# Low parts of the second layer's attention weights on GpSimd: one instruction of full width, or two of half width

## The chip, the cores and the metric

The kernel runs on one core of one Trainium2 chip. The metric is the device time of one execution in microseconds (us); three runs of the kernel before gave 1139.0, 1139.27 and 1141.51 us, with a median of 1139.27. The core has five engines that run their own instruction queues in order and wait for one another by semaphores: TensorE (PE, matmuls and transposes), VectorE (DVE), ScalarE (ACT), GpSimd (POOL), and SyncE (SP), which issues most DMAs.

## The reference

Two layers work on 512 tokens of width 1024. Each layer norms its input, projects it (`w_in`), mixes tokens, adds four heads of cross-attention into 256 memory tokens, projects back (`w_out`), and ends with a gated feed-forward part. The first layer mixes by retention, the second by differential attention, six heads with two softmaxes each:

```python
h = rms_norm(x, attn_norm_w[layer])
u = h @ w_in[layer]
# layer 1: q, k (6 heads, 2 x 64), v (6 heads, 128), qc (4 memory heads)
sc = q k^T * scale - slope * |t - s|           # masked by chunks of 64
p = softmax(sc)                                # per head: two maps
o = rms_norm((p[0] - lam * p[1]) @ v, diff_subln_w)
o_mem = memory_attention(qc, mk, mv)
x = x + concat(o, o_mem) @ w_out[layer]
x = x + (silu(gate) * up) @ w_down[layer]      # feed-forward
```

All inputs and weights are float32.

## The kernel before

TensorE is fed with numbers of reduced precision (`fp32r`). To keep the accuracy of float32, each operand is kept as two tiles, a high part H (a rounded copy) and a low part L (the rest), and each product is three matmuls: H·H, H·L, L·H (`mm3`). A weight is loaded by SP into a tile `wr` of 128x1024 (three buffers, `load_chunk`), ACT copies it into `wh`, and another engine writes `wl` = `wr` - `wh`. Three buffers each of `wh` and `wl` hold three such chunks.

Which engine makes the low part is decided in `split_chunk`: VectorE for most weights, GpSimd for the chunks of the second layer's `w_in` (20 of them) and the first five of its `w_out`. One of these five lies in two tiles of 768 and 256 columns, so GpSimd has 26 such instructions, nearly all 128x1024. When the low part is out, the chunk is put into `staged`, from which the matmul code takes it, and the load of the chunk three further on is issued.

GpSimd also computes the reciprocal roots of the norms (`power`, an instruction on 4 or 8 columns, in the profile `sm<-sm,mhalf`), which stand in the same queue.

In the second layer's attention (`diff_layer`), PE's main line is the projection of blocks of 512 tokens with one chunk of weights after the other. Between these matmuls side streams place their work: the norm of queries and keys (ACT square, DVE sum, GpSimd root, DVE product, PE transpose, ACT and DVE split into H and L), the scores (`ps<-qk,qk`), their softmax (a fused DVE pass over each of the two score banks, two ACT exponentials, a DVE combination `wk<-wk,sm,wk`), its transposes (`ps<-ident,wk`), the product with v (`ps<-wk,v`), and at the end of a head its norm and transpose (`ps<-ident,zo`), after which ACT writes the head's H tile and DVE its L tile. The output projection (`out_proj`) takes heads 0 to 3 first, then the memory heads, then heads 4 and 5.

The order of all instructions is fixed when the program is built. A planner (`Weave`) keeps a modelled clock for each engine. Each stream is a Python generator: when it yields, it is put back into a heap with a due time (by default `W.cur`, the modelled end of what it has issued plus a hand-over), and whenever PE's modelled clock has passed a due time, that stream goes on and emits its next instructions. If PE's code asks for something that isn't there yet (`Store.at`), the planner steps the side streams until it is, and only then emits PE's next matmul. A different due time of one stream therefore reorders the streams after it, on all engines. All instructions have the same line in the profile (289), since a helper emits them; they are told apart by tile names: `ps` is a PSUM bank, `wk` a work tile, `qk` a query, key or head tile, `zo` a head's output while it is normed, `sm` a few columns of sums.

Of the kernel before, what the change touches and what calls it, by code (L numbers as in the profile page):

```python
# [15 lines left out]
ALU = mybir.AluOpType  # L16
# [278 lines left out]
def body(ctx: ExitStack, tc: tile.TileContext, x_d, mem_d, w_d, par_d, dec_d, ali_d, out_d):  # L295
# [4 lines left out]
    W = Weave()  # L300
    V, A, G = Engine(W, "dve", nc.vector), Engine(W, "act", nc.scalar), Engine(W, "pool", nc.gpsimd)
# [9 lines left out]
    def page(tag, shape, bufs, dt=F32):  # L311
        z = sb.tile(shape, dt, tag=tag, name=nm(tag), bufs=bufs)
        W.page(tag, bufs, region(z[:, 0:1])[0])
        return z
# [60 lines left out]
    def f(ap):  # L375
        return ap.bitcast(F32)
# [54 lines left out]
    def split_h(dH, src, scale=None):  # L431
        if scale is None:
            A.activation(dH, src, AF.Copy)
        else:
            A.activation(dH, src, AF.Copy, scale=scale)

    def split_l(dH, dL, src, scale=None):
        if scale is None:
            V.tensor_tensor(dL, src, f(dH), op=ALU.subtract)
        else:  # L440
            V.scalar_tensor_tensor(dL, src, scale, f(dH), op0=ALU.mult, op1=ALU.subtract)
# [38 lines left out]
    def load_chunk(i):  # L480

        if i in loaded or i >= RING:
            return
        n = SPECS[i][4] * len(SPECS[i][5])
        raw = page("wr", [P, CW], 3)
        parts = 2 if i < 4 else 1
        cuts = [slice(j * n // parts, (j + 1) * n // parts) for j in range(parts)]
        for s in cuts:
            DMA.dma_start(raw[:, s], w_d[i][:, s])
            if i == 0:  # L490
                DMA.dma_start(xT[cuts.index(s)], x_d[cuts.index(s)])
        loaded[i] = raw, cuts, n
# [3 lines left out]
    def begin(i):  # L496

        if i not in begun and i < RING and SPECS[i][0][0] != "st":
            begun.add(i)
            if i < 3:  # L500
                load_chunk(i)
            W.add(split_chunk(i))

    def split_chunk(i):
        while i not in loaded:
            yield 0.3
        raw, cuts, n = loaded[i]
        key = SPECS[i][0]
        d = key[2] - NOUT + 1 if key[0] == "out" else -1
        if d in (0, 1):  # L510

            while (key[1], d) not in left:
                yield 0.5
            tag, n_page, bufs = (("qc", CW, 2), ("v", MAIN, 8))[d]
        else:
            tag, n_page, bufs = None, CW, 3
        if n_page < n:
            cuts = [slice(0, n_page), slice(n_page, n)]
        pages = [[page(tag or z, [P, n_page], bufs, F32R) for z in ("wh", "wl")] for _ in range(-(-n // n_page))]
        W.cur = max(W.ready(raw[:, 0:1]), W.ready(pages[0][0][:, 0:1]) - 0.2)  # L520
        yield
        for s in cuts:
            wH, wL = [z[:, s.start % n_page:(s.stop - 1) % n_page + 1] for z in pages[s.start // n_page]]
            split_h(wH, raw[:, s])
            yield
            if key[1] == 1 and (key[0] == "in" or key[0] == "out" and key[2] <= NOUT):
                G.tensor_tensor(wL, raw[:, s], f(wH), op=ALU.subtract)
            else:
                split_l(wH, wL, raw[:, s])
        kk, w = SPECS[i][4], n // SPECS[i][4]  # L530
        staged[i] = [[pages[k * w // n_page][j][:, k * w % n_page:k * w % n_page + w] for k in range(kk)] for j in range(2)]
        load_chunk(i + 3)
# [1216 lines left out]
```

## Time and profile before

| | us |
|---|---|
| median of three runs | 1139.27 |
| profiled execution, its device time | 1139.37 |
| its span from first to last instruction | 1137.3 |
| PE busy in the span | 1127.1 (99%) |
| DVE busy | 852.4 (75%) |
| ACT busy | 624.6 (55%) |
| POOL busy | 215.6 (19%) |

The span and what lies around it (2.07 us) make the device time. The ends of matmuls in the records are modelled, so two matmuls that follow one another overlap in the list, and the rate of PE is read from start to start. The granted TensorE clock is full in all of the span. The second layer's attention, with its output projection, lies between about 560 and 760 us; the feed-forward part of the first layer ends before it, that of the second follows.

### The profile page before, as it was taken

To read this page: it belongs to the slowest core of one execution; us is meant where nothing else is said; L and a number is where in the kernel's file an instruction comes from. 1 tells how busy PE (TensorE), PEld (TensorE's weight loads), DVE (VectorE), ACT (ScalarE), POOL (GpSimd) and SP (SyncE) were. 2 spreads that over 40 slices of the span, in tenths; PEclk is the share of its full clock that TensorE was granted. 3 is DMA by queue.
4 is the path that set the end of the run, shared out by engine and by line. 5 is a ranking of instruction groups with operands and counts; after the bars stand their busy time and mean duration, and the time that the engine had idled before them with its cause. 6 is when DMAs were issued, how large, how long until landed. Compare 5 with 4: busy or idle time off the path is not lost.

```text
span 1137.3 us, 18765 instructions
## 1 busy us (share of the span) xinstructions
PE 1127.1 (99%) x6917; PEld 996.6 (88%) x6917; DVE 852.4 (75%) x1648; ACT 624.6 (55%) x1291; POOL 215.6 (19%) x174
## 2 busy tenths in 40 slices
PE   9999999999999999999999999999999999999998
PEld 7788888889999999998888777888899999999987
DVE  6769895788886677877557587957989877677862
ACT  6557863545564445555466566746555544455541
POOL 0120010311111011100353553344111111001100
PEclk9999999999999999999999999999999999999999
DMA  6341122357775566654231321122656766556532
GB/s 227 130 148 65 47 93 82 119 135 199 198 206 160 167 157 176 172 149 160 77 109 56 112 75 50 45 74 93 175 167 172 214 170 184 149 162 181 151 111 76
DMA packets 68491, 153.42 MB, mean 135 GB/s; under 512 B 7728, under 2 KB 20400, under 8 KB 68400
## 3 DMA queue, kind: packets, MB, share of 16 engines
q1 hardware_dynamic: 57312, 132.28, 35.6%
q0 software_dynamic: 10944, 19.93, 11.0%
q8 instruction: 54, 0.88, 0.3%
q14 instruction: 37, 0.30, 0.1%
q10 hardware_dynamic: 144, 0.03, 0.0%
HBM read 150.10 MB, written 2.10 MB: 134 GB/s over the span
## 4 chain that ended last, share of the span: by engine, by line
PE 91%; ACT 3%; DVE 3%; issue 1%; DMA 0%; SPq 0%; DVEq 0%; ACTq 0%
PE ps L289 91%; DVE wk L289 1%; ACT wk L289 1%; ACT wh L289 1%; DVE sm L289 1%; ACT qk L289 1%; DVE qk L289 0%; DMA wr<-w_t 0%; ACT mkY L289 0%; DVE mkL L289 0%; SPq L289 0%; ACT tab L289 0%; ACT qc L289 0%; ACT L289 0%; ACT xw L289 0%
## 5 line engine op out<-in xcount | busy, mean ns | idle before, releaser
L289 PE MATMUL ps<-xw,wh 128*128 128x256 f32 (+1 forms) x1032 | 211.6, 326 | 0.0
L289 ACT ACTIVATE wk<-ps 128x256 f32<-128x256 f32 (+3 forms) x214 | 90.5, 426 | 184.1 <-PE ps L289 183.2
L289 PE MATMUL ps<-xw,wl 128*128 128x256 f32 (+1 forms) x948 | 179.0, 306 | 0.0
L289 PEld LDWEIGHTS ps<-xw,wh 128*128 128x128 f32 x1032 | 154.4, 190 | 15.5
L289 POOL DMA_DIRECT2D wk<-w_t x76 | 67.8, 1002 | 463.8 <-DMA wk<-w_t 176.0
L289 PE MATMUL ps<-wh,xw 128*128 128x512 f32 (+1 forms) x512 | 149.1, 370 | 1.0 <-DVE qk L289 1.0
L289 PEld LDWEIGHTS ps<-xw,wl 128*128 128x128 f32 x948 | 131.2, 190 | 7.4
L289 PE MATMUL ps<-qk,wl 128*128 128x512 f32 (+1 forms) x528 | 135.6, 386 | 0.0
L289 ACT ACTIVATE wh<-wr 128x512 fp32r<-128x512 f32 (+1 forms) x144 | 118.7, 827 | 28.6 <-PE ps L289 16.3
L289 DVE TENSOR_TENSOR wl<-wk,wl 128x512 fp32r<-128x512 f32 (+3 forms) x150 | 94.2, 628 | 41.3 <-ACT wl L289 40.8
L289 DVE TENSOR_TENSOR wh<-wk,wh 128x512 fp32r<-128x512 f32 (+3 forms) x130 | 79.2, 609 | 48.7 <-ACT wh L289 48.5
L289 PEld LDWEIGHTS ps<-qk,wl 128*128 128x128 f32 x528 | 96.1, 188 | 18.3
L289 PE MATMUL ps<-v,wh 128*128 128x256 f32 x792 | 106.1, 279 | 0.0
L289 PEld LDWEIGHTS ps<-wh,xw 128*128 128x128 f32 x512 | 91.5, 188 | 15.8 <-DVE qk L289 1.4
L289 PE MATMUL ps<-qk,wh 128*128 128x512 f32 (+1 forms) x393 | 104.3, 387 | 0.5 <-DVE qk L289 0.5
L289 ACT ACTIVATE wl<-wk 128x512 fp32r<-128x512 f32 (+3 forms) x150 | 85.5, 570 | 31.0 <-DVE wk L289 17.0
L289 PEld LDWEIGHTS ps<-v,wh 128*128 128x128 f32 x792 | 98.3, 189 | 0.0
L289 PE MATMUL ps<-wl,xw 128*128 128x512 f32 (+1 forms) x256 | 94.9, 371 | 0.4 <-DVE wl L289 0.4
L289 DVE TENSOR_TENSOR xT<-ps,xT 128x512 f32<-128x512 f32 (+1 forms) x81 | 55.1, 681 | 51.7 <-PE ps L289 51.4
L289 ACT ACTIVATE wh<-wk 128x512 fp32r<-128x512 f32 (+3 forms) x130 | 72.6, 558 | 34.1 <-DVE wk L289 24.6
L289 PEld LDWEIGHTS ps<-qk,wh 128*128 128x128 f32 x393 | 71.9, 188 | 15.6 <-DVE qk L289 1.1
L289 PE MATMUL ps<-v,wl 128*128 128x256 f32 x576 | 77.4, 279 | 0.0
(169 smaller groups left out, 1956.5 us busy)
## 6 DMA issues: line engine op xcount, KB each, us to landing
wr<-w_t SPq DMA_DIRECT2D x148, 512.0 KB, 3.6
wk<-w_t SPq DMA_DIRECT2D x108, 256.0 KB, 4.0
wk<-w_t POOLq DMA_DIRECT2D x76, 256.0 KB, 6.1
wk<-w_t SPq DMA_DIRECT2D x48, 192.0 KB, 4.6
wk<-w_t SPq DMA_DIRECT2D x32, 128.0 KB, 4.4
wr<-w_t SPq DMA_DIRECT2D x8, 256.0 KB, 5.1
xT<-x_t SPq DMA_DIRECT2D x8, 256.0 KB, 5.1
zo<-mem_t SPq DMA_DIRECT2D x8, 256.0 KB, 5.0
```

The costliest lines, as they stand in the source:

```text
L289: return call(out, *args, **kw)
```

## The change

Each low part that GpSimd makes is written by two instructions, each on half of the columns. After each half the stream yields until the modelled end of that half, so other streams may place instructions between the halves and behind them, and the chunk is put into `staged` (and the load of the chunk three further on is issued) after the modelled end of the second half, where before both came with the instruction's issue.

```diff
             split_h(wH, raw[:, s])
             yield
             if key[1] == 1 and (key[0] == "in" or key[0] == "out" and key[2] <= NOUT):
-                G.tensor_tensor(wL, raw[:, s], f(wH), op=ALU.subtract)
+
+                for j in range(2):
+                    z = slice(j * wL.shape[1] // 2, (j + 1) * wL.shape[1] // 2)
+                    G.tensor_tensor(wL[:, z], raw[:, s][:, z], f(wH)[:, z], op=ALU.subtract)
+                    W.cur = W.last
+                    yield
             else:
                 split_l(wH, wL, raw[:, s])
```

The order changes from the second layer's first input chunk on and is the same again, but for tile numbers, from the fifth output tile of that layer's `w_out` to the end. PE's list has as many matmuls as before; GpSimd's has 26 instructions more. Three places follow, near the end of the attention, where the last heads and the output projection meet.

The first is GpSimd's queue there, before: `wl_1610_7952` is the low part of the first output chunk, `wl_1696_8343`, `qc_1700_8347` and `wl_1698_8345` are those of the next three, and `sm` rows with 128x4 are roots of head norms.

```order
L289 TENSOR_TENSOR wl_1610_7952<-wr_1509_7598,wh_1609_7951 128x1024
L289 TENSOR_TENSOR sm_1601_7930<-sm_1600_7929,mhalf_73 128x8
L289 TENSOR_TENSOR sm_1622_7974<-sm_1621_7973,mhalf_73 128x8
L289 TENSOR_TENSOR sm_1674_8251<-sm_1673_8250,mhalf_73 128x4
L289 TENSOR_TENSOR wl_1696_8343<-wr_1539_7712,wh_1695_8342 128x1024
L289 TENSOR_TENSOR qc_1700_8347<-wr_1628_8013,qc_1699_8346 128x1024
L289 TENSOR_TENSOR wl_1698_8345<-wr_1574_7858,wh_1697_8344 128x1024
L289 TENSOR_TENSOR sm_1740_8512<-sm_1739_8511,mhalf_73 128x4
```

The same place in GpSimd's queue of the changed kernel, where `wl_1608_7966`, `wl_1708_8391`, `qc_1712_8395` and `wl_1710_8393` are these chunks:

```order
L289 TENSOR_TENSOR wl_1608_7966<-wr_1507_7608,wh_1607_7965 128x512
L289 TENSOR_TENSOR sm_1612_7980<-sm_1611_7979,mhalf_73 128x8
L289 TENSOR_TENSOR wl_1608_7966<-wr_1507_7608,wh_1607_7965 128x512
L289 TENSOR_TENSOR sm_1630_8080<-sm_1629_8079,mhalf_73 128x4
L289 TENSOR_TENSOR sm_1695_8360<-sm_1694_8359,mhalf_73 128x4
L289 TENSOR_TENSOR wl_1708_8391<-wr_1526_7700,wh_1707_8390 128x512
L289 TENSOR_TENSOR qc_1712_8395<-wr_1641_8133,qc_1711_8394 128x512
L289 TENSOR_TENSOR wl_1708_8391<-wr_1526_7700,wh_1707_8390 128x512
L289 TENSOR_TENSOR wl_1710_8393<-wr_1595_7925,wh_1709_8392 128x512
L289 TENSOR_TENSOR qc_1712_8395<-wr_1641_8133,qc_1711_8394 128x512
L289 TENSOR_TENSOR wl_1710_8393<-wr_1595_7925,wh_1709_8392 128x512
L289 TENSOR_TENSOR sm_1739_8510<-sm_1738_8509,mhalf_73 128x4
```

Three whole subtractions in a row became six halves in a row, halves of two chunks alternate, and a root now stands between the halves of the first output chunk.

The second place is PE where the first output tile takes head 3, before: `ps_1691_8326<-ident_66,zo_1669_8237` (20 rows ahead of the first of these) was that head's transpose, and `qk_1693_8338` and `qk_1694_8339` are its H and L tiles; `ps_1720_8402` and `ps_1721_8403` are score banks of the last head.

```order
L289 MATMUL ps_1720_8402<-qk_1617_7959,qk_1613_7955 128x384
L289 MATMUL ps_1721_8403<-qk_1617_7959,qk_1613_7955 128x384
L289 MATMUL ps_1720_8402<-qk_1618_7960,qk_1613_7955 128x384
L289 MATMUL ps_1721_8403<-qk_1618_7960,qk_1613_7955 128x384
L289 MATMUL ps_1720_8402<-qk_1617_7959,qk_1614_7956 128x384
L289 MATMUL ps_1721_8403<-qk_1617_7959,qk_1614_7956 128x384
L289 MATMUL ps_1692_8336<-qk_1625_8002,wh_1609_7951 128x512
L289 MATMUL ps_1692_8336<-qk_1624_8001,wl_1610_7952 128x512
L289 MATMUL ps_1692_8336<-qk_1693_8338,wh_1609_7951 128x512
L289 MATMUL ps_1692_8336<-qk_1694_8339,wh_1609_7951 128x512
L289 MATMUL ps_1692_8336<-qk_1693_8338,wl_1610_7952 128x512
```

The same place on PE in the changed kernel, with head 3's transpose in the second row (`zo_1686_8333`), its tiles `qk_1723_8460` and `qk_1724_8461`, and the score banks `ps_1728_8466` and `ps_1729_8467` of the last head:

```order
L289 MATMUL ps_1718_8442<-ident_66,wk_1673_8264 128x128 x3
L289 MATMUL ps_1719_8447<-ident_66,zo_1686_8333 128x128 x4
L289 MATMUL ps_1702_8383<-qk_1664_8232,wl_1608_7966 128x512
L289 MATMUL ps_1728_8466<-qk_1591_7913,qk_1587_7909 128x512
L289 MATMUL ps_1729_8467<-qk_1591_7913,qk_1587_7909 128x512
L289 MATMUL ps_1728_8466<-qk_1592_7914,qk_1587_7909 128x512
L289 MATMUL ps_1729_8467<-qk_1592_7914,qk_1587_7909 128x512
L289 MATMUL ps_1728_8466<-qk_1591_7913,qk_1588_7910 128x512
L289 MATMUL ps_1729_8467<-qk_1591_7913,qk_1588_7910 128x512
L289 MATMUL ps_1730_8478<-ident_66,wk_1720_8454 128x128 x4
L289 MATMUL ps_1702_8383<-qk_1723_8460,wh_1607_7965 128x512
L289 MATMUL ps_1702_8383<-qk_1724_8461,wh_1607_7965 128x512
```

Before, 27 rows of other work stood between the head's transpose and the first use of its tiles; now eight do, six of them the scores of the last head.

The third place is DVE's queue at the same point, before, where `qk_1694_8339` is head 3's L tile and an `ISA` row with `tab` is the fused pass over a score bank:

```order
L289 SCALAR_TENSOR_TENSOR wk_1660_8210<-wk_1661_8211,sm_1679_8269,wk_1660_8210 128x512
L289 RECIPROCAL sm_1686_8290<-sm_1686_8290 128x1
L289 SCALAR_TENSOR_TENSOR sm_1687_8291<-s0_1682_8278,der_89,sm_1686_8290 128x1
L289 SCALAR_TENSOR_TENSOR wk_1683_8279<-wk_1684_8280,sm_1687_8291,wk_1683_8279 128x128
L289 SCALAR_TENSOR_TENSOR qk_1694_8339<-ps_1691_8326,der_89,qk_1693_8338 128x512
L289 ISA wk_1683_8279,sm_1701_8351<-ps_1704_8354,tab_1627_8007 128x256
```

And in the changed kernel, with `qk_1724_8461` as head 3's L tile:

```order
L289 TENSOR_TENSOR zo_1686_8333<-ps_1682_8303,sm_1695_8360 128x512
L289 SCALAR_TENSOR_TENSOR v_1196_6271<-ps_1666_8235,r_1182_6214,v_1195_6270 128x256
L289 RECIPROCAL sm_1714_8400<-sm_1714_8400 128x1
L289 SCALAR_TENSOR_TENSOR sm_1715_8401<-s0_1672_8263,der_89,sm_1714_8400 128x1
L289 SCALAR_TENSOR_TENSOR wk_1703_8385<-wk_1704_8386,sm_1715_8401,wk_1703_8385 128x384
L289 SCALAR_TENSOR_TENSOR sm_1731_8483<-s0_1631_8088 128x4
L289 ISA wk_1705_8387,sm_1725_8463<-ps_1728_8466,tab_1622_8033 128x512
L289 ISA sm_1725_8463 128x1
L289 ISA wk_1706_8388,sm_1725_8463<-ps_1729_8467,tab_1622_8033 128x512
L289 ISA sm_1725_8463 128x1
L289 TENSOR_TENSOR wk_1722_8457<-ps_1718_8442,wk_1721_8456 128x384
L289 SCALAR_TENSOR_TENSOR qk_1724_8461<-ps_1719_8447,der_89,qk_1723_8460 128x512
```

Now the fused passes over the score banks `ps_1728_8466` and `ps_1729_8467` and one more subtraction stand ahead of head 3's L tile.

## Rows read from the trace of the kernel before

**Rows 1.** Page, busy time, share of the span and instructions of each engine.

```profile
PE 1127.1 (99%) x6917; PEld 996.6 (88%) x6917; DVE 852.4 (75%) x1648; ACT 624.6 (55%) x1291; POOL 215.6 (19%) x174
```

**Rows 2.** Busy time by stretch: stretch, PE, PEld, DVE, ACT, POOL, clock, DMA, GB/s.

```profile
130.00:520.00 390.00, 390.00 (x2529) 355.68 (x2529) 305.09 (x556) 207.18 (x406) 50.77 (x50) 1.00 0.55 152
...
560.00:760.00 200.00, 197.40 (x1178) 162.57 (x1177) 142.52 (x371) 127.25 (x316) 93.50 (x52) 1.00 0.25 80
```

**Rows 3.** PE's waits from 560 to 760 us: total, times, longest.

```profile
PE ps L289 <- DVE qk L289: 1.0, 1, 1.0
PE ps L289 <- DVE wk L289: 0.7, 2, 0.5
PE ps L289 <- ACT wk L289: 0.6, 3, 0.2
PE ps L289 <- ACT sm L289: 0.2, 1, 0.2
```

**Rows 4.** Timeline of PE: start, us, instruction, in brackets idle time and releaser.

```profile
654.72 0.44 PE L289 MATMUL ps<-ident,wk 128*128 128x128 f32 x2 [0.15 <-DVE wk L289]
...
679.12 0.40 PE L289 MATMUL ps<-wl,xw 128*128 128x512 f32 x1
679.35 0.40 PE L289 MATMUL ps<-wh,xw 128*128 128x512 f32 x1
680.74 0.50 PE L289 MATMUL ps<-wh,xw 128*128 128x512 f32 x1 [1.00 <-DVE qk L289]
...
742.26 0.96 PE L289 MATMUL ps<-qk,qk 64*128 64x512 f32 x6
743.15 1.57 PE L289 MATMUL ps<-wk,v 128*128 128x256 f32 x12
...
745.54 0.60 PE L289 MATMUL ps<-ident,wk 128*128 128x128 f32 x4
745.89 0.48 PE L289 MATMUL ps<-zo,wl 128*128 128x512 f32 x1
...
755.55 0.65 PE L289 MATMUL ps<-ident,wk 128*128 128x128 f32 x4
...
759.96 0.60 PE L289 MATMUL ps<-ident,zo 128*128 128x128 f32 x4
```

**Rows 5.** GpSimd's groups by form, 560 to 760 us: shapes, count | busy, mean ns | idle.

```profile
L289 POOL TENSOR_TENSOR wl<-wr,wh 128x1024 fp32r<-128x1024 f32 x23 | 55.2, 2400 | 67.1 <-ACT wh L289 67.1
...
L289 POOL TENSOR_TENSOR tab<-tab,tab 128x512 f32<-128x512 f32 x1 | 1.3, 1295 | 3.5 <-ACT tab L289 3.5
```

**Rows 6.** Timeline of GpSimd, two places.

```profile
676.83 2.39 POOL L289 TENSOR_TENSOR wl<-wr,wh 128x1024 fp32r<-128x1024 f32 x1
...
741.65 2.41 POOL L289 TENSOR_TENSOR qc<-wr,qc 128x1024 fp32r<-128x1024 f32 x1
744.00 2.41 POOL L289 TENSOR_TENSOR wl<-wr,wh 128x1024 fp32r<-128x1024 f32 x1
```

**Rows 7.** Timeline of DVE, at and near those places.

```profile
653.92 0.22 DVE L289 SCALAR_TENSOR_TENSOR sm<-s,der,sm 128x1 f32<-128x1 f32 x1
...
678.22 1.02 DVE L289 SCALAR_TENSOR_TENSOR sm<-s,der,sm 128x1 f32<-128x1 f32 x1
...
679.94 0.75 DVE L289 SCALAR_TENSOR_TENSOR qk<-ps,der,qk 128x512 fp32r<-128x512 f32 x1
...
743.13 0.95 DVE L289 SCALAR_TENSOR_TENSOR sm<-s,der,sm 128x1 f32<-128x1 f32 x1
744.12 2.58 DVE L289 SCALAR_TENSOR_TENSOR wk<-wk,sm,wk 128x256 f32<-128x256 f32 x1
...
746.62 0.68 DVE L289 CUSTOM_DVE_ANT_0 wk<-ps,tab 128x512 f32<-128x512 f32 x1
...
748.89 0.55 DVE L289 TENSOR_TENSOR wk<-ps,wk 128x384 fp32r<-128x384 f32 x1
```

## The prediction, made before the changed kernel ran

> **What bounds the kernel now.** I read the page first: PE is busy for 1127.1 of 1137.3 us [rows 1], so all its idle time is 10.2 us, and no change on another engine can give more. Then the busy time by stretch: from 130 to 520 us, the feed-forward part of the first layer, PE is never idle, while the second layer's attention, 560 to 760 us, has 2.6 us of idle PE (200 less 197.40) [rows 2]. The change touches only that stretch, so what it gives or takes is what happens to those 2.6 us. PE's waits there are seven, 2.5 us in sum: one of 1.0 for a DVE tile, two for DVE's work tiles, three of about 0.2 for ACT, one of 0.2 [rows 3]. The bracket of a wait understates it, since matmul ends are modelled: from 679.35 to 680.74 is 1.39 us, where the matmul before had 0.23 (679.12 to 679.35), so this wait cost 1.16, not 1.00 [rows 4]. With about 0.17 more for each of the seven, the stretch holds some 3.7 us of waits. That is the most the change could give back. POOL is busy for 93.5 of the 200 us [rows 2], and PE waits for it nowhere [rows 3].
>
> **The change part by part.** *GpSimd's own time.* 26 subtractions become 52. A full one takes 2.40 us; one of 512 columns is shown by a sum of norms, 1.295 [rows 5]. Two halves are 2.59, so 0.19 more for each pair and 4.9 us for 26. This lies on an engine that is idle for half of the stretch and for which PE never waits. A chunk's low part is due two chunks ahead of its use, and a chunk is 24 matmuls of 0.23 [rows 4], so 11 us of cover for 2.6 us of work. I cost it at 0; if that cover were gone, one chunk would cost at most a half, 1.3. The loads behind the halves go out about 2.6 us later, three chunks (16 us) ahead of need: also 0.
>
> *DVE behind GpSimd.* In the trace some DVE instructions last until a GpSimd instruction ends. The small product `sm<-s,der,sm` takes 0.22 alone (653.92), but the one at 678.22 took 1.02 and ended at 679.24, just when the subtraction of 676.83 + 2.39 ended, at 679.22 [rows 6, 7]. That is 0.80 lost on DVE, and the tile that PE waits for at 680.74 is the DVE row of 679.94, which ends at 680.69, two instructions further down that queue [rows 4, 7]. With halves such a stop ends at 1.3 at the latest, where it was 2.4. The Trainium skill states this as a rule (page "SBUF — State Buffer", section "SBUF: two separate sides"): a port pair shared by VectorE and GpSimd goes to one of them for a whole instruction, and the other is shut out. The trace agrees, with the 1.02 against 0.22 above; by the rule alone the halves would only help.
>
> *The reordering.* This is the larger part, since the due times have moved. I followed the orders past the waits of before.
> - At 680.74 PE began a new bank that DVE had still to empty. In the new order the four new banks of that block come after the old scores, with more work between a bank's last reader and its reuse. I take this wait as gone: -1.2; bounds -1.2 and 0.
> - At 654.72 PE waits 0.15, with the cost of restarting about 0.3, for the softmax of the first head, two tiles of 256 columns; the new order puts about 0.9 us more of PE work between these scores and their transposes: -0.3; bounds -0.3 and 0.
> - The three small waits for ACT are transposes of a finished head right behind six scores, and in the new order two of them stand in the same place and a third a little closer. The two early waits for the memory queries move, but DVE's queue before them moves as well. 0 for all; bounds -1.5 and +1.0.
> - New is the place in the output projection where PE takes head 3. Between the head's transposes and its first use now stand a projection matmul, the six scores of the last head and four transposes. PE takes the H tile in order, and then needs the L tile `qk_1724_8461`. On DVE this tile stands behind both fused passes over these very scores and one subtraction of 384 columns. From the end of the scores: 0.1 until DVE starts, 2 x 0.61 for the passes (0.68 each in the row, less the overlap of records), 0.47 for the subtraction (0.55 in the row), 0.75 for the tile, 0.05 to PE: 2.6 [rows 7]. PE in that time has four transposes, 0.35 (745.54 to 745.89), and one matmul of 0.23: 0.6 [rows 4]. It waits 2.0. Before, 27 rows stood there and PE did not wait. Bounds 1.0 (if an earlier wait of PE takes part of it) and 2.9.
> - Ahead of it, head 3's transpose needs DVE's product `zo_1686_8333`, which stands behind a combination of two work tiles, and this now meets the six halves of GpSimd. Such a combination was held to 2.58 at 744.12, by the subtraction of 744.00 [rows 6, 7]. A half holds it for 1.3 at most, 0.65 in the middle. The last head's norm has one matmul less to hide behind than before: its chain took 755.55 to 759.96 with no wait [rows 4], so 0.2. Together +0.8; bounds 0 and 2.8.
>
> The sum is -1.2 - 0.3 + 0 + 2.0 + 0.8 = +1.3 us. Against the profiled execution's own time of 1139.37 this is 1140.7. That execution lies 0.1 above the median of the runs shown, which I leave in.
>
> **Rivals.** *Halves give more than the order takes.* DVE is freed sooner everywhere; head 3's tile comes as DVE's queue is ahead, and the waits of before go. For it: 24 long subtractions in this stretch and several DVE rows held by them. Against it: only one of PE's seven waits is traced to such a row, and the passes ahead of head 3's tile follow scores, not GpSimd. It gives up to 3.7: with two thirds of that, 2.5, the time is 1136.9.
>
> *DVE held twice at the output projection.* Six halves in a row occupy GpSimd for 6 x 1.3 = 7.8 us, and two combinations of work tiles (`wk_1673_8264`, `wk_1703_8385`) stand on DVE ahead of head 3's product and L tile. If each is held for a whole half, the two cost 2.6 where I counted 0.65, which makes +3.2 and 1142.6. From 0.9 us more than I counted the kernel is slower by over 0.2%. For it: 743.13 and 744.12, two DVE rows held one after the other by successive subtractions (0.95, then 2.58) [rows 6, 7]. Against it: the planner also models this exclusion, and puts such rows where its clock sees GpSimd free.
>
> *The halves act as one.* The second half follows so closely that DVE gets no turn between; the stops stay at 2.6 and the change does nothing for DVE but add 0.19 each. For it: GpSimd's rows at 741.65 and 744.00 overlap in the record by 0.06. Against it: the DVE row of 743.13 ended at 744.08, at that seam, and the next was held by the next subtraction [rows 6, 7], so DVE does get in. Then the wait at 680.74 would come back for the half of it that is the stop, 0.8 x 0.75 = 0.6, and the time is 1141.3. The skill has a sentence that speaks for this one (page "GPSIMD Engine Reference", section "2.1 Instruction dispatch"): a GpSimd core begins the next instruction when its own share of the last is done, without waiting for the others. The row of 743.13 speaks against it as far as DVE's turn goes.
>
> **How the numbers follow.** What a measurement of this kernel can tell from no change is 0.2%, 2.3 us: 1137.0 to 1141.55. The forecast, near 1140.7, has 0.52; its own range is 1139.4 to 1141.9, which lies mostly within that. The first rival has 0.12, the second 0.24, the third 0.12. Faster by over 0.2%: about half of the first rival, 0.06. Slower by over 0.2%: a tenth of the forecast, three quarters of the second rival and a third of the third, 0.05 + 0.18 + 0.04 = 0.27. The rest, 0.67, is no change. For 8 in 10 I take 1138.0 to 1143.0: it leaves out most of the first rival and the far end of the second.
>
> **What would show it.** In the profile after: PE's wait of 1.0 for a DVE `qk` tile between 675 and 685 is gone, and a new one of about 2 us for a DVE `qk` tile stands near 745, right behind six scores of 512 columns; GpSimd's subtractions show near 1.3 us and 52 times (half the width), with DVE rows held for no more than about 1.3 us beside them; POOL's busy time is near 220. The forecast is wrong if PE's idle time from 560 to 760 us comes out under 2.6 us or over 5 us, or if PE waits for GpSimd's `wl` at all.

## The result and the profile after

The changed kernel is slower: 1146.34 us median of four executions (1144.63 to 1146.56), against 1139.41 of the kernel before on the same chip (four executions). The ratio is 1.0054, 95% interval 1.0042 to 1.0066. The forecast was 1140.7 with a range up to 1143.0, so the time lies outside it, on the slow side. The profiled execution took 1146.12 us with a span of 1144.3, 7.0 longer than before.

The page's first line of the changed kernel (columns as in [rows 1]), and then its busy times by stretch (columns as in [rows 2], the first to be read against the second line there):

```profile
PE 1129.7 (99%) x6917; PEld 999.1 (87%) x6917; DVE 848.9 (74%) x1648; ACT 624.2 (55%) x1291; POOL 219.8 (19%) x200
```

```profile
560.00:760.00 200.00, 193.07 (x1146) 159.96 (x1145) 137.27 (x368) 125.85 (x315) 95.24 (x75) 0.98 0.25 77
740.00:744.00 4.00, 2.19 (x19) 1.68 (x17) 3.53 (x6) 3.88 (x9) 4.00 (x4) 1.00 0.00 0
744.00:748.00 4.00, 1.18 (x9) 0.58 (x5) 4.00 (x8) 1.81 (x5) 3.45 (x3) 1.00 0.61 175
748.00:750.00 2.00, 1.35 (x6) 1.26 (x6) 1.90 (x6) 0.40 (x2) 0.54 (x1) 0.53 0.92 293
750.00:752.00 2.00, 2.00 (x8) 1.71 (x7) 1.19 (x2) 0.00 (x0) 0.47 (x1) 0.50 0.40 152
752.00:754.00 2.00, 2.00 (x7) 1.41 (x6) 0.00 (x0) 0.00 (x0) 0.00 (x0) 0.50 0.00 0
754.00:756.00 2.00, 2.00 (x14) 1.95 (x13) 0.29 (x1) 0.92 (x3) 0.00 (x0) 0.77 0.00 0
```

GpSimd has 26 instructions more and 4.2 us more of busy time. PE's idle time from 560 to 760 us is 6.9 us, where it was 2.6; 4.6 of it lie in the eight microseconds from 740 to 748, and 0.65 right behind them. There the granted clock, full until then, falls to 0.50: the lower of the two levels, 1.2 GHz. PE's waits in the same stretch, but for one of 0.2 (us in total, times, longest; before: [rows 3]):

```profile
PE ps L289 <- DVE qk L289: 3.5, 1, 3.5
PE ps L289 <- DVE v L289: 1.8, 1, 1.8
PE ps L289 <- ACT sm L289: 0.8, 1, 0.8
PE ps L289 <- DVE wk L289: 0.4, 1, 0.4
```

The timeline of PE shows the two long ones (columns as in [rows 4]):

```profile
742.12 0.33 PE L289 MATMUL ps<-wk,v 128*128 128x128 f32 x1 [1.81 <-DVE v L289]
...
743.40 0.96 PE L289 MATMUL ps<-qk,qk 64*128 64x512 f32 x6
744.29 0.66 PE L289 MATMUL ps<-ident,wk 128*128 128x128 f32 x4
744.70 0.47 PE L289 MATMUL ps<-qk,wh 128*128 128x512 f32 x1
748.64 0.80 PE L289 MATMUL ps<-qk,wh 128*128 128x512 f32 x1 [3.47 <-DVE qk L289]
...
751.80 0.63 PE L289 MATMUL ps<-zo,wl 128*128 128x512 f32 x1
752.23 1.05 PE L289 MATMUL ps<-zo,wh 128*128 128x512 f32 x2
```

The matmul of 748.64 is the one that takes head 3's L tile, behind the six scores of the last head: the place that the prediction named. From start to start it came 3.94 us after the one ahead of it, so the wait cost 3.7 where 2.0 was forecast. The one of 742.12 cost 2.0. At the end a matmul of 512 columns takes 0.43 from start to start (751.80 to 752.23), where it takes 0.23 at full clock. Why both waits are so long is seen on GpSimd and DVE beside them, GpSimd first:

```profile
739.48 1.31 POOL L289 TENSOR_TENSOR wl<-wr,wh 128x512 fp32r<-128x512 f32 x1 [1.20 <-ACT wh L289]
740.74 1.46 POOL L289 TENSOR_TENSOR qc<-wr,qc 128x512 fp32r<-128x512 f32 x1
742.16 2.53 POOL L289 TENSOR_TENSOR wl<-wr,wh 128x512 fp32r<-128x512 f32 x2
744.65 1.57 POOL L289 TENSOR_TENSOR qc<-wr,qc 128x512 fp32r<-128x512 f32 x1
746.18 1.27 POOL L289 TENSOR_TENSOR wl<-wr,wh 128x512 fp32r<-128x512 f32 x1
```

```profile
739.67 1.40 DVE L289 SCALAR_TENSOR_TENSOR wk<-wk,sm,wk 128x256 f32<-128x256 f32 x1
...
741.59 0.47 DVE L289 SCALAR_TENSOR_TENSOR v<-ps,r,v 128x256 fp32r<-128x256 f32 x1
...
742.66 0.80 DVE L289 SCALAR_TENSOR_TENSOR sm<-s,der,sm 128x1 f32<-128x1 f32 x1
743.49 1.61 DVE L289 SCALAR_TENSOR_TENSOR wk<-wk,sm,wk 128x384 f32<-128x384 f32 x1
745.02 1.22 DVE L289 SCALAR_TENSOR_TENSOR sm<-s 128x4 f32<-128x4 f32 x1
746.16 0.68 DVE L289 CUSTOM_DVE_ANT_0 wk<-ps,tab 128x512 f32<-128x512 f32 x1
...
747.86 0.73 DVE L289 SCALAR_TENSOR_TENSOR qk<-ps,der,qk 128x512 fp32r<-128x512 f32 x1
```

Four DVE rows are held until a half ends, and do their own work then: the one of 739.67 (its half ends at 740.79), that of 742.66 (743.42, the middle of the pair of 742.16), that of 743.49 (744.69), and that of 745.02, which ends at 746.24, just when the half of 744.65 does, at 746.22. Undisturbed rows of these shapes take 0.49, 0.22, 0.62 and 0.15. DVE loses 3.6 us here. The six halves follow one another without a gap; DVE gets in at four of the five seams, and its next row of this kind finds the next half begun. The fused passes over the last head's scores, which were ready at 744.4, start at 746.16.

Summed from start to start over the second layer's attention, counting what exceeds the usual distance of such matmuls by over 0.25 us: the waits of before come to 4.1 us, and those that the changed kernel has left of them to 2.3, so 1.8 were given back. The two new waits take 5.7, the low clock takes 3.1 (0.47 x 1.4 from 748.64 to 750, 0.50 x 4, 0.23 x 2), and small lags 0.3. That is +7.3; the start of the kernel happened to be 0.4 shorter.

### The profile page after: what moved, and what is told of

The parts are those of the page before. It is cut to its first block, busy times and chain, and to the rows that moved or that the text cites. A ratio compares the mean times of both kernels' runs of the same rounds, so it can differ in the third digit from the quotient of the medians.

```text
span 1144.3 us, 18813 instructions
## 1 busy us (share of the span) xinstructions
PE 1129.7 (99%) x6917; PEld 999.1 (87%) x6917; DVE 848.9 (74%) x1648; ACT 624.2 (55%) x1291; POOL 219.8 (19%) x200
## 4 chain that ended last, share of the span: by engine, by line
PE 89%; DVE 5%; ACT 4%; issue 1%; POOL 0%; DMA 0%; SPq 0%; DVEq 0%
PE ps L289 89%; DVE wk L289 2%; ACT wk L289 1%; DVE sm L289 1%; ACT wh L289 1%; DVE qk L289 1%; ACT qk L289 0%; DMA wr<-w_t 0%; SPq L289 0%; POOL sm L289 0%; ACT tab L289 0%; POOL wl L289 0%; ACT L289 0%; ACT xw L289 0%; DVE tab L289 0%
## 5 line engine op out<-in xcount | busy, mean ns | idle before, releaser
L289 ACT ACTIVATE wk<-ps 128x256 f32<-128x256 f32 (+4 forms) x214 | 90.3, 426 | 189.7 <-PE ps L289 188.8
```

Of the source, the lines that this page charges most:

```text
L289: return call(out, *args, **kw)
```

## The experiments

The theory (A): at the output projection DVE is held again and again by GpSimd's queue of subtractions, in an order in which head 3's tile is needed too soon, and the idle time that this makes on PE lowers its clock. The rivals: (B) the split itself costs; (C) the order costs whatever GpSimd does. Four kernels separate them; seven more then look for the place and the part of the change.

**The split alone, in the order of before.** The planner is told of one whole subtraction, two halves are issued:

```diff
-                G.tensor_tensor(wL, raw[:, s], f(wH), op=ALU.subtract)
+                W.run("pool", 0.17 + 0.0021 * free_size(wL), [wL], [raw[:, s], f(wH)], True)
+                for j in range(2):
+                    z = slice(j * wL.shape[1] // 2, (j + 1) * wL.shape[1] // 2)
+                    nc.gpsimd.tensor_tensor(wL[:, z], raw[:, s][:, z], f(wH)[:, z], op=ALU.subtract)
```

> Each of GpSimd's 26 subtractions is issued as two halves back to back, while every other instruction stays in the order of before (the planner is told of one whole instruction, and stages the chunk as before). Theory A (the loss is DVE held again and again by the queue of halves at the output projection, in the new order, and TensorE's lower clock after the idle time that this makes): the order of before has no such place, so the time is that of before or a little under, 1138.3 to 1139.8, and the wait of PE near 680 (1.2 us from start to start) shrinks by up to 0.6. Theory B (two instructions instead of one hold DVE longer wherever they stand): 1142 or more, with PE's waits grown over the whole attention. Theory C (the order alone): as before, 1139.4.

Measured: 1139.33 us, ratio to before 0.9998 (0.9989 to 1.0007). B falls. The wait near 680 did not shrink (idle for 1.1, where it was 1.0 before). GpSimd and DVE ahead of it:

```profile
677.28 2.54 POOL L530 TENSOR_TENSOR wl<-wr,wh 128x512 fp32r<-128x512 f32 x2
...
678.67 1.18 DVE L289 SCALAR_TENSOR_TENSOR sm<-s,der,sm 128x1 f32<-128x1 f32 x1
```

The small product arrived just behind the seam and was held for nearly the whole second half: 1.18, where the whole subtraction had held it for 1.02 [rows 7]. A half is a smaller limit for a stop, but it did not make this one shorter.

**The order alone.** In the order of the changed kernel, the whole subtraction is issued in the place of the second half:

```diff
-                    G.tensor_tensor(wL[:, z], raw[:, s][:, z], f(wH)[:, z], op=ALU.subtract)
+                    W.run("pool", 0.17 + 0.0021 * free_size(wL[:, z]), [wL[:, z]], [raw[:, s][:, z], f(wH)[:, z]], True)
+                    if j == 1:
+                        nc.gpsimd.tensor_tensor(wL, raw[:, s], f(wH), op=ALU.subtract)
```

> The order of the changed kernel on every engine, but GpSimd issues each subtraction whole, at the place of its second half, and nothing at the place of the first. Theory A: three whole subtractions in a row (7.2 us) stand where six halves stood, and DVE's rows there are held again, in fewer and longer stops; the waits near 740 and 745 stay, 4 to 8 us in sum, and the clock falls behind them: 1144 to 1149. Theory B (it is the split itself): the time falls to about 1140. Theory C (the new order alone, whatever GpSimd does): 1146, unchanged within 1.

Measured: 1151.0 us (1149.69 to 1153.33), ratio 1.0103 (1.009 to 1.0117), 2 above what A allowed. DVE at the same place:

```profile
745.27 2.48 DVE L289 SCALAR_TENSOR_TENSOR wk<-wk,sm,wk 128x256 f32<-128x256 f32 x1
...
748.85 1.14 DVE L289 SCALAR_TENSOR_TENSOR sm<-s,der,sm 128x1 f32<-128x1 f32 x1
750.02 2.69 DVE L289 SCALAR_TENSOR_TENSOR wk<-wk,sm,wk 128x384 f32<-128x384 f32 x1
```

Against undisturbed rows these are stops of 2.0, 0.9 and 2.1 us, where the halves made 0.9, 0.6 and 1.0 of them and, on a fourth row, 1.1. PE's longer waits from 560 to 775 us in this run:

```profile
PE ps L289 <- DVE wk L289: 4.7, 4, 1.5
PE ps L289 <- DVE v L289: 2.9, 1, 2.9
PE ps L289 <- DVE qk L289: 2.1, 1, 2.1
```

The last two lines are this place: 5.0 us, where the halves left 5.3 (1.8 and 3.5), so here whole subtractions made PE wait no longer than halves (between the two waits PE also ran at the lower clock, 0.57 from 750 to 754). In this order halves are 4.7 us better all the same, by the medians, and the first line shows where most of it lies: four waits for work tiles, at 578, 625, 715 and 725 us, in place of one of 0.4. Ahead of the second and the fourth, DVE rows were held by whole subtractions too (undisturbed, four rows of the first kind take 1.14 and the other takes 0.22):

```profile
618.73 5.46 DVE L289 TENSOR_SCALAR wk<-wk,sm 128x256 f32<-128x256 f32 x4
...
721.58 1.83 DVE L289 SCALAR_TENSOR_TENSOR sm<-s,der,sm 128x1 f32<-128x1 f32 x1
```

It is the order that loses; GpSimd's queue has a part in how much, and not only at this place.

**The order without GpSimd's last halves.** Low parts of output chunks 1 to 3 are not computed, PE reads the high part in their place (the lines that hand it over are left out here):

```diff
-                    G.tensor_tensor(wL[:, z], raw[:, s][:, z], f(wH)[:, z], op=ALU.subtract)
+                    if key[0] == "out" and key[2] in (1, 2, 3):
+                        W.run("pool", 0.17 + 0.0021 * free_size(wL[:, z]), [wL[:, z]], [raw[:, s][:, z], f(wH)[:, z]], True)
+                    else:
+                        G.tensor_tensor(wL[:, z], raw[:, s][:, z], f(wH)[:, z], op=ALU.subtract)
```

> The changed kernel in its order, but the low parts of output chunks 1, 2 and 3 are not computed: PE reads the high part in their place, and GpSimd's six halves from 739 to 747 us are gone. Theory A: the four DVE rows that were held there (1.40, 0.80, 1.61, 1.22 us) come down to 0.49, 0.22, 0.62 and 0.15; the wait near 740 falls from 2.0 to about 1.0, that near 745 from 3.7 to about 2.0, which is what order alone leaves; 1143.4 if the clock still falls, 1140.3 if it doesn't. Theory B: 1140 as well, with the waits gone altogether. Theory C (order alone): the waits stay 2.0 and 3.7, and the time 1146.

Measured: 1141.27 us (1140.34 to 1143.52), ratio 1.0018 (1.0009 to 1.0027). PE and DVE there:

```profile
741.28 0.33 PE L289 MATMUL ps<-wk,v 128*128 128x128 f32 x1 [0.91 <-DVE v L289]
...
744.00 0.49 PE L289 MATMUL ps<-qk,wh 128*128 128x512 f32 x1
746.09 0.50 PE L289 MATMUL ps<-qk,wh 128*128 128x512 f32 x1 [1.59 <-DVE qk L289]
```

```profile
742.74 0.22 DVE L289 SCALAR_TENSOR_TENSOR sm<-s,der,sm 128x1 f32<-128x1 f32 x1
742.99 0.62 DVE L289 SCALAR_TENSOR_TENSOR wk<-wk,sm,wk 128x384 f32<-128x384 f32 x1
743.53 0.15 DVE L289 SCALAR_TENSOR_TENSOR sm<-s 128x4 f32<-128x4 f32 x1
```

The rows fall to 0.22, 0.62 and 0.15, the waits to 1.1 and 1.9 from start to start, and the mean clock of this trace is 1.000. So of the 5.7 us of new waits, about 2.9 are the order's and 2.8 GpSimd's hold on DVE; and without the hold the clock did not fall in the profiled execution. In four of the eleven it did somewhere: their mean clock is 0.998 or 0.999, and they took 1142.0 to 1143.5, the others 1140.3 to 1141.6.

**PE kept busy in the long wait.** Fourteen repeats of the matmul ahead of it (`fill` is 14 for head 3 in the first output tile of the second layer, else 0); head 3's high product is so counted 15 times in that tile (shown in part):

```diff
             TE.matmul(out, lhsT=l_, rhs=r_, start=start and i == 0, stop=stop and i == 2, skip_group_check=resume)
+            for _ in range(fill if i == 0 else 0):
+                nc.tensor.matmul(out, lhsT=l_, rhs=r_, start=False, stop=False, skip_group_check=resume)
```

> The changed kernel, with 14 more matmuls of 512 columns on PE in the long wait near 745 (a repeat of the one that stands ahead of it, so head 3's high product is counted 15 times in the first output tile). They take 14 x 0.227 = 3.2 us of a wait of 3.7. If the lower clock from 748.6 to 755 us comes from PE having been idle, it stays at full there and the time falls by the 3.1 us that the matmuls lost at the lower clock: about 1143.2. If the clock falls for another reason (the load of DVE and DMA at that moment, say), the time stays 1146. If the filler itself delays PE, it is longer than 1146.

Measured: 1144.8 us (1144.57 to 1145.79), half of the way to 1143.2. In its trace (this execution lay 2.5 us later here; its clock was also low near its start, 0.65 from 24 to 28 us) the place shows:

```profile
747.57 3.38 PE L411 MATMUL ps<-qk,wh 128*128 128x512 f32 x14
751.21 0.51 PE L289 MATMUL ps<-qk,wh 128*128 128x512 f32 x1 [0.26 <-DVE qk L289]
```

```profile
750.00:752.00 2.00, 1.74 (x11) 1.19 (x9) 1.97 (x7) 0.97 (x4) 0.04 (x1) 1.00 0.95 279
```

With matmuls in the wait, and DVE and DMA as loaded as before, the clock stays at full. That fits a fall that comes from PE's idle time, and speaks against the load as its cause; it is one trace, and the last section shows that a fall behind a wait is not certain. The other four executions have a mean clock of 0.999 (the changed kernel 0.997, the profiled one of this run 0.998), so they too may have lost a shorter stretch, which may be the other half of the way; where, is not shown.

**Which part of the change makes the order.** Two kernels have halves or late staging, but nothing between the halves: halves without any yield, and whole subtractions with the yield and the staging behind them.

```diff
                     G.tensor_tensor(wL[:, z], raw[:, s][:, z], f(wH)[:, z], op=ALU.subtract)
-                    W.cur = W.last
-                    yield
```

> Two half-width subtractions each, of which the planner knows, but no yield after either: other streams can't come between, and the chunk is staged at once. In the order so made, head 3's transposes stand 22 rows ahead of the first use of its tiles, where the changed kernel has 8, and GpSimd's halves of one chunk follow one another. If the loss of the changed kernel comes from the one place where head 3 is taken too early, this one is near the kernel before: 1138.5 to 1140.5. If any other order than that of before costs some us (the order before being a lucky one), 1141 to 1144. If the second instruction itself costs, 1142 or more.

```diff
                 G.tensor_tensor(wL, raw[:, s], f(wH), op=ALU.subtract)
+                W.cur = W.last
+                yield
```

> The kernel before with one part of the change alone: whole subtractions, but the stream yields until the modelled end and stages the chunk only then. The order is a third one, with 46 rows between head 3's transposes and their first use. If staging late is what costs (chunks and loads come too late), this one is 2 us or more slower than before, over 1141.5, and PE waits for a weight tile. If the yield between the halves is what made the bad place, it is near before: 1138.5 to 1140.5.

Measured: 1138.99 us both, ratios 0.9997 (0.9988 to 1.0006) and 0.9998 (0.999 to 1.0007): no change, though both have orders of their own. So not every other order loses, neither part costs by itself, and PE's longest wait is 1.2 in either. Then two kernels with one yield of the two: only the one behind both halves,

```diff
                 for j in range(2):
                     z = slice(j * wL.shape[1] // 2, (j + 1) * wL.shape[1] // 2)
                     G.tensor_tensor(wL[:, z], raw[:, s][:, z], f(wH)[:, z], op=ALU.subtract)
-                    W.cur = W.last
-                    yield
+                W.cur = W.last
+                yield
```

> The changed kernel without the yield between the two halves; the one behind the second half, with the late staging, stays. The halves of one chunk follow one another on GpSimd. The order so made is a fourth one, and has head 3's transposes only 6 rows ahead of the first use of its tiles, with two fused passes, two combinations of work tiles and two more passes ahead of its low tile on DVE. If it is that place which decides, PE waits there 2.5 to 4.5 us and the time is 1141 to 1146, although no stream comes between the halves. If the yield between the halves is what harms, it is near before: 1138.5 to 1140.5.

and only the one between them:

```diff
-                    W.cur = W.last
-                    yield
+                    if j == 0:
+                        W.cur = W.last
+                        yield
```

> The changed kernel without the yield behind the second half, so that the chunk is staged as soon as that half is issued; the yield between the halves stays. The order is that of the changed kernel but for a few rows. If the late staging has no part in the loss, the time is that of the changed kernel, 1145 to 1147, with the waits of 2.0 and 3.7 near 740 and 745 and the low clock behind them. If staging late is a part of it, 1140 to 1143.

Measured: 1147.51 us (1146.02 to 1149.69, ratio 1.007, 1.0057 to 1.0083) and 1146.55 (1144.96 to 1146.84, ratio 1.0057, 1.0043 to 1.0071). The first is 1.5 above its range, and it is the telling one: nothing comes between its halves, but its order too takes head 3 a few rows behind its transposes. PE there, and DVE:

```profile
744.24 0.50 PE L289 MATMUL ps<-qk,wh 128*128 128x512 f32 x1 [1.93 <-ACT qk L289]
748.15 0.79 PE L289 MATMUL ps<-qk,wh 128*128 128x512 f32 x1 [3.41 <-DVE qk L289]
```

```profile
741.92 1.00 DVE L289 SCALAR_TENSOR_TENSOR sm<-s,der,sm 128x1 f32<-128x1 f32 x1
742.96 1.72 DVE L289 SCALAR_TENSOR_TENSOR wk<-wk,sm,wk 128x512 f32<-128x512 f32 x1
...
745.74 1.30 DVE L289 SCALAR_TENSOR_TENSOR sm<-s,der,sm 128x1 f32<-128x1 f32 x1
```

The first wait is for head 3's H tile, which ACT begins only at 743.52, behind other work of its own; the second is for the L tile, and again three DVE rows ahead of it are held until a half ends. So where head 3 is taken decides, not which yield put it there.

**Head 3 taken later, in the changed kernel.** Once with heads 4 and 5 at the end of the output projection, once only behind the two memory heads:

```diff
-    out_proj(1, *outs, [0, 1, 2, 3], norms[3])
+    out_proj(1, *outs, [0, 1, 2], norms[3])
```

> The changed kernel with one other thing: the output projection of the second layer takes head 3 with heads 4 and 5 at its end, and no longer among the first four. The wait of 3.7 us near 745 then has some 20 matmuls in front of it and goes; the wait of 2.0 near 740 is not touched. If the clock falls because of the long idle time, it stays at full: 1146.1 - 3.7 - 3.1 = 1139.3, the time of before. If the clock falls after the first wait too, or because the load is high there, 1142.4. If the wait only moves to the next tile that DVE makes (the softmax of the last head), 1144 or more.

```diff
         early = [(h, oT, h) for h in early] + [(H + i, om, i) for i in range(2)]
+        if layer == 1:
+            early = early[:3] + early[4:] + early[3:4]
```

> The changed kernel, where the first output tiles take head 3 behind the two memory heads and not ahead of them: six matmuls of 0.23 us come in front of the wait near 745, which falls from 3.7 to 2.4. By the wait alone 1144.7; if the shorter idle time keeps the clock at full, 1141.7 (the wait of 1.6 in the run without GpSimd's last halves kept it at full, that of 3.5 in the changed kernel did not).

Measured: 1141.27 us (1139.48 to 1141.96), ratio 1.0015 (1.0006 to 1.0023), and 1142.3 (1141.95 to 1144.26), ratio 1.0026 (1.0016 to 1.0035). In the first the long wait is gone (PE's waits near the place: one of 1.8 for `v`). But the clock now falls behind that wait of 1.8:

```profile
743.00:744.00 1.00, 1.00 (x6) 0.60 (x3) 0.96 (x2) 1.00 (x3) 1.00 (x2) 0.54 0.00 0
744.00:745.00 1.00, 1.00 (x5) 0.83 (x6) 1.00 (x1) 0.41 (x1) 1.00 (x2) 0.50 0.52 53
745.00:746.00 1.00, 1.00 (x6) 0.39 (x3) 1.00 (x2) 0.00 (x0) 1.00 (x1) 0.50 0.68 242
746.00:747.00 1.00, 1.00 (x7) 0.91 (x6) 1.00 (x4) 0.29 (x1) 1.00 (x2) 0.76 0.57 229
```

That is 1.7 us lost. Of its eleven executions three have a mean clock of 1.000 and took 1139.5 to 1139.9, the forecast; the other eight have 0.998 or 0.999 and took 1141.0 to 1142.0. In the second the wait fell to 0.7 from start to start, less than the 2.4 expected, because the scores ahead of it ran at the lower clock (0.50 from 744 to 746) and so gave DVE time.

**Both remedies together**, head 3 late and no halves at the end (high part in place of the low part, as above):

> The two remedies together: head 3 is taken late, and GpSimd's six halves at the output projection are left out (PE reads the high part of output chunks 1 to 3 in place of the low part). The wait near 745 is gone, that near 740 is the 1.1 of the run without the halves, and the clock stays at full. If these two places and the clock are all that the new order costs, the time is 1141.3 - 1.9 = 1139.4, or up to 0.8 less where nothing else is lost: 1138.6 to 1139.6. If something else in the new order costs, it stays over 1140.

Measured: 1138.73 us (1138.33 to 1140.92), ratio 0.9995 (0.9986 to 1.0004). The longest of PE's waits from 560 to 775 us:

```profile
PE ps L289 <- DVE v L289: 0.9, 1, 0.9
```

With those two things taken away nothing else in the new order costs. No kernel that computes everything came out faster than the one before by more than these runs can tell.

## Why the prediction was wrong

**Right:** what bounds the kernel, and GpSimd's own time (4.9 forecast for 26 instructions more, 4.2 measured, waited for nowhere). The wait of 680.74 is gone, as taken (-1.2); the others that were to stay or go came to another -0.6, forecast -0.3. The new wait stands at head 3's L tile, behind the last head's scores. Without GpSimd it is 1.9 against the 2.0 of the sum, shown by the run without the last halves. The sign set for a wrong forecast, PE idle for over 5 us, came: 6.9.

**The step that failed** is the last term of the sum: "A half holds it for 1.3 at most, 0.65 in the middle ... Together +0.8". It counted one stop. There were four, by 0.9, 0.6, 1.0 and 1.1 us, and on PE they cost 2.8. The stops are not independent draws from the middle of a half. Three of them followed one another: DVE is released when a half ends, its next row with its operands in SBUF comes at once (743.49 after 743.46, 745.02 after 745.10 less the overlap of records), the next half has just begun, and it is held for most of that one (1.0 of 1.27, 1.1 of 1.57). The rival "DVE held twice at the output projection" (0.24) had the mechanism, and nearly its condition, that each stop lasts a whole half. Its ground against, that the planner models the exclusion, fell: the planner's clock did not keep these rows apart. The first wait, at 742.12, belongs to this term too, but at another tile than head 3's transpose: the v tile on DVE, behind the first held row. Even without the last halves 1.1 of that wait stay, which the new order makes by itself and for which the sum had nothing.

**What no term had** is, besides that 1.1, the clock, 3.1 us. The trace of before shows it full in its whole span, so nothing there had a price for it; but a wait of 2 us forecast right behind other waits was reason to ask, and the range should have carried it. The second rival's 1142.6 with 3.1 more is 1145.7, near what was measured, though that rival had two stops in place of four.

**The port.** The Trainium skill's rule (page "SBUF — State Buffer", section "SBUF: two separate sides") was read as speaking for the halves: held for an instruction, so shorter instructions, shorter stops. The trace agrees with the rule itself, down to the ends of the stops (743.46 against 742.16 + 2.53/2). But behind a stop comes a new one while GpSimd's queue is full: beside 8.0 us of halves (739.48 to 747.45) the stops came to 3.6 us, beside 7.2 of whole ones (745.07 to 752.29) to 5.0, and PE's two waits there came to 5.3 and 5.0. In the old order halves gave nothing (0.9998); in the new one they gave 4.7 us over whole ones, most of it at other places than this.

**The other rivals.** That halves give more than the order takes did not come. That the halves act as one is refuted: DVE has a row in at four of the five seams of the six halves.

## What to carry to other kernels

When a change moves a due time in a planner, look for the consumers that come a few rows behind their producers in the new order, and price them with every other queue that stands on the producer's engine just then: one such place, with the clock behind it, cost these 7 us, while two other reorderings, without such a place, cost nothing. A run of instructions on GpSimd with no gap between them can hold VectorE again and again, each time for much of an instruction (0.6 to 1.1 us beside halves of 1.3, 0.9 to 2.1 beside whole ones of 2.4); splitting them made single stops shorter, but in these two traces it took nothing off PE's waits beside the run. What did was to take head 3 later and to leave the run out. And where PE is nearly always busy, a forecast wait of a few us can have the lower clock behind it as a second price.

## What the runs showed of the hardware that was not expected

- The clock's fall is not settled by the wait ahead of it. Up to 744 us the changed kernel and the one with head 3 late have the same order on PE, with the same wait of 1.8 us. In the one profile the clock stays at 1.00 until 748, in the other it is 0.54 from 743 to 744; and three of eleven executions of the latter show no fall. With the waits 0.9 and 1.6 of the run without the last halves the trace shows none either, but four of its eleven executions have a lower mean clock. Nor does a fall need this place: the kernel before, whose trace shows none, took 1141.2 to 1141.8 in eight of the 68 executions run beside the experiments, each with a mean clock of 0.998 or 0.999, and the traces of two other kernels show the lower clock near their start (the run with the filler, 0.65 from 24 to 28 us, and the one with the yield behind both halves, 0.60 from 8 to 12).
- The lower clock pays for itself in part where PE runs ahead of DVE: in the kernel with head 3 behind the memory heads it left a wait of 0.7 where 2.4 was expected. Its two executions with a mean clock of 1.000 took 1142.5 and 1142.9, no less than the median of 1142.3.
- GpSimd is held by DVE as well, it seems: halves of 512 columns take 1.26 where two follow one another (2.53 for both), but 1.46 and 1.57 where a DVE row of 256 or 384 columns got in ahead of them (740.74, 744.65).
- A product on one column, 128x1 with three operands in SBUF, is held like one of 384 columns (0.22 to 1.18 us in the run with halves in the old order).
